# Hybrid decoder block on one core: two recurrence chains, three tile sets for combining the inverse's blocks, and an earlier load of the norm's weight

## The chip, the cores and the metric

The kernel runs on one core of one Trainium2 chip. The metric is the device time of one execution in microseconds; the time of a kernel is the median of its runs. The engines are named as the profile names them: PE multiplies matrices (PEld loads its weights), DVE works element by element, ACT does activations and copies, POOL does the rest of the elementwise work, and SP issues most of the DMA transfers.

## What is computed

One layer for 1024 tokens of width 1024. `h = rmsnorm(x)`, one projection `h @ w_in`, and three branches: a gated delta rule with 8 heads, stick-breaking attention with 8 heads, and a cross attention into 256 memory tokens with 4 heads. Each branch is projected to width 1024, the three are gated and added, and an output projection, the residual and a last norm follow.

The delta rule is what most of the change is about. Per head, in chunks of 64 tokens:

```python
t_inv = triangular_solve(eye + m, eye)          # m strictly lower triangular, 64 x 64
u = t_inv @ (v * beta);  w = t_inv @ (k * beta * exp(G))
a_intra = (q @ k.T) * gam_incl
def step(s, xs):                                # one chunk
    v_new = u_n - w_n @ s
    o = q_n @ s + a_n @ v_new
    s = s * exp(last_n) + k_n.T @ v_new
    return s, o
```

## The kernel before

All numbers are float32; matrices that need full precision are split into two parts, and a product is three matmuls (`mm3`, L156). The kernel joins two chunks into one of 128 tokens: it inverts the two 64x64 diagonal blocks of every chunk for all heads at once and adds the off-diagonal block from them. There are `NT` = 8 chunks of 128 tokens and `H` = 8 heads.

The stages, in order of time:

1. **Start, A.** Rows of x (128 tokens each) are loaded by `row` (L268), normed (`norm`, L273, whose last instruction, L284 on DVE, needs the norm's weight `g1`), transposed on PE (L292) and split (L143 on ACT, L144 on DVE). L364 to L372 set the order in which SP is given the first loads: rows 0 and 4 of x, two pieces of `wv0`, the weight `g1` broadcast to 128 partitions, two more pieces of `wv0`.
2. **Projections.** `stream` (L170) works through a list of jobs. Every `slot()` runs one unit of 12 matmuls; other work is put between the slots by generators and a `pacer` (L848), which calls a generator so often that it has done a given share of its steps. Beside the projections run `solver` (the 64x64 inverses, on DVE), `memory` (the cross attention) and `combine`.
3. **combine (L742).** For each head: three loads into `t12` and `ct` (L747 to L749), eight small matmuls Y (L752), a scaling on DVE (L753), eight matmuls X (L758), a copy on ACT (L759) and a store (L760). The tiles carry the tags `tmp` and `T1` in a pool with one buffer each, so one set of tiles serves all heads in turn. Y and X share the PSUM tag `wk` (2 banks) with the scores and values of `memory`.
4. **Attention** with the rest of the projections between its parts.
5. **Merge.** `branch` (L1150) runs for the memory branch (`y_ym`, 8 times), the attention branch (`y_ysb`, 8 times) and the delta branch (`y_ydn`, 8 times). The recurrence is put between the matmuls of the first two: `beside3` is called 40 times and has `recurrence` do all its steps by then (`RECUR` = 65, `RP` = 1.05). What is left is called at `recur(2.0)` (L1200). `y_ydn` reads the results `odn` of the recurrence. `load_o(wout, ...)` (L1205) loads and splits the last weight, `wo`, beside it.
6. **Output** projection, residual and norm (L1213 on).

**recurrence (L765)** goes through chunks `n` and, in each, groups `g` of four heads. A step (n, g) has four parts with a `yield` after each:

- loads; `kS` = k times the state S (L801, PE), `vb` += r3 * kS (L803, DVE, four instructions)
- `Tr` = inverse times vb (L809, PE), copied to `vn` (L811, ACT)
- `o` from q and S (L816) and from the inner attention and vn (L817), then `dS` = k times vn (L821), then the new S on DVE (L824)
- the norm of o (L834 on ACT, L835 to L837 on POOL, L838 on DVE), transposes `oT` (L841), product with the gate `zt` (L842, DVE), split into `odn`

The two groups share no values, but the code runs group 0 and then group 1 of a chunk, and they share buffers: `kd`, `qd`, `zt`, `vn` and `sq` have one, `kt`, `vb` and `at` two, and the PSUM tag `wk` has three banks (L1188).

The order on each engine is fixed when the program is built (`TileContext(nc, schedule_with_timeline_sim=True)`, L1316); it is not the order of the source. In the profile, SP issues the load of L393 between those of L153.

Of the kernel before, what the change touches and what calls it, by code (L numbers as in the profile page):

```python
# [11 lines left out]
F32 = mybir.dt.float32  # L12
F32R = mybir.dt.float32r
AF = mybir.ActivationFunctionType
ALU = mybir.AluOpType
# [4 lines left out]
P = 128  # L20
T = 1024
NT = 8
KC = 8
H = 8
# [13 lines left out]
def hybrid_block(ctx, tc, x, mem, norm_g, mem_norm_g, wq, wv0, wba, convw, a_log, dt_bias,  # L38
# [17 lines left out]
    cst = pool("cst", 1)  # L56
# [25 lines left out]

    ident = cst.tile([P, P], F32, name="ident")
    make_identity(nc, ident)
    tri = cst.tile([P, P], F32, name="tri")
    gp.memset(tri, 1.0)
    gp.affine_select(out=tri, in_=tri, compare_op=ALU.is_ge, fill=0.0, base=0,
                     pattern=[[1, P]], channel_multiplier=-1)
    ones = cst.tile([P, P], F32, name="ones")
    gp.memset(ones, 1.0)  # L90
    mhalf = cst.tile([P, 8], F32, name="mhalf")
    gp.memset(mhalf, -0.5)
    cw = cst.tile([P, 24, 4], F32, name="cw")
# [174 lines left out]
    def row(src, tb):  # L268
        t = ap_.tile([P, T], F32, tag="xt", bufs=4, name=f"xt_{tb}")
        sy.dma_start(out=t, in_=src[0, tb * P:tb * P + P, :])  # L270
        return t
# [89 lines left out]
        sums("S1", "S2")  # L361
        return functools.partial(sums, "S3", "S4")

    rows_ = {tb: row(x, tb) for tb in (0, 4)}  # L364

    w0 = [vp_.tile([P, KC, 272], F32R, name=f"w0{j}") for j in "hl"]
    w0r = [raw_unit(f"v0_{j}", wv0[j]) for j in range(2)]
    g1 = ap_.tile([P, T], F32, name="g1")
    sy.dma_start(out=g1, in_=norm_g.rearrange("a b -> (a b)").partition_broadcast(P))
    w0r += [raw_unit(f"v0_{j}", wv0[j]) for j in range(2, 4)]  # L370
    rb = vp_.tile([P, KC, 16], F32, name="rb")
    sy.dma_start(out=rb, in_=wba.rearrange("p (a b) -> p a b", a=KC))  # L372
# [23 lines left out]
    v_st.close()  # L396


    beta, G, nG, eG, elast, dec = (tab(n) for n in ("beta", "G", "nG", "eG", "elast", "dec"))
    nr2, r1, r3, eq = tab("nr2"), tab("r1"), tab("r3"), tab("eq")  # L400
    SS = dict(c=None)

# [221 lines left out]
    def solver():  # L624
        vp = slv["pool"] = pool("solve", 1, side="right", stack=solve_st)
        o = psum("tr", "nr2T")
        pe.transpose(o[0:64, 0:P], nr2.rearrange("p h n -> p (h n)"), ident)
        nrs = vp.tile([64, P], F32, name="nrs")
        ve.tensor_copy(nrs, o[0:64, 0:P])
        for b in range(2):  # L630
            sy.dma_start(out=nr_d[b], in_=nrs[:, b * 64:b * 64 + 64])
        nrp = vp.tile([P, 64], F32, name="nrp")
        sy.dma_start(out=nrp, in_=nr_d.rearrange("b m i -> (b m) i"))

        M = vp.tile([P, 64, 64], F32, name="M")
        sy.dma_start(out=M, in_=md_d.rearrange("b h n j i -> (b h n) j i"))
        tmp = vp.tile([P, 1024], F32, name="tmp")
        yield
        for c in range(4):
            s = slice(c * 16, c * 16 + 16)  # L640
            ve.tensor_tensor(out=M[:, s, :], in0=M[:, s, :], in1=nrp.unsqueeze(1).to_broadcast([P, 16, 64]),
                             op=ALU.mult)
        gp.memset(M.rearrange("p k r -> p (k r)")[:, 0:4096:65], 1.0)
        yield
        for j in range(1, 63):
            b = 63 - j
            t = tmp[:, 0:j * b].rearrange("p (k r) -> p k r", k=j)
            ve.tensor_tensor(out=t, in0=M[:, 0:j, j].unsqueeze(2).to_broadcast([P, j, b]),  # L648
                             in1=M[:, j, j + 1:64].unsqueeze(1).to_broadcast([P, j, b]), op=ALU.mult)
            d = M[:, 0:j, j + 1:64]  # L650
            ve.tensor_tensor(out=d, in0=d, in1=t, op=ALU.add)  # L651
            yield
        gp.dma_start(out=td_d.rearrange("b h n j i -> (b h n) j i"), in_=M)
        for c in range(4):
            s = slice(c * 16, c * 16 + 16)
            t = vp.tile([64, 16, 64], F32, tag=("tmp", "T1")[c % 2], name=f"T1_{c}")
            ve.tensor_copy(t, M[0:64, :, s].rearrange("p k r -> p r k"))
            sy.dma_start(out=t1_d[:, :, s, :].rearrange("h n r k -> (h n) r k"), in_=t)
            yield
            yield  # L660
# [79 lines left out]
                yield  # L740

    def combine():  # L742
        vp = slv["pool"]
        for h in range(H):
            t, u = (vp.tile([P, 2, 512], F32, tag=n, name=f"{n}c_{h}") for n in ("tmp", "T1"))
            t12, ct, Y, X = (v.rearrange("p (n k) -> p n k", n=NT) for v in (t[:, 0], t[0:64, 1], u[:, 0], u[0:64, 1]))
            sy.dma_start(out=t12[0:64], in_=t1_d[h].rearrange("n r k -> r n k"))  # L747
            sy.dma_start(out=t12[64:P], in_=td_d[1, h].rearrange("n k r -> k n r"))
            sy.dma_start(out=ct, in_=mo_d[h])  # L749
            o = psum("wk", f"Y_{h}")  # L750
            for n in range(NT):
                pe.matmul(o[64:P, n * 64:n * 64 + 64], ct[:, n, :], t12[0:64, n, :], start=True, stop=True)  # L752
# [12 lines left out]
    def recurrence(ep, odn):  # L765
# [10 lines left out]
        def loads(n, g):  # L776
            kt = ld(kt_d, n, g, "kt") if n else None
            vb = ld(vb_d, n, g, "vb")
            tt, hs = tts[g], slice(g * 4, g * 4 + 4)
            for b in range(2):  # L780
                q = slice(b * 64, b * 64 + 64)
                sy.dma_start(out=tt[q, :, q], in_=td_d[b, hs, n].rearrange("h j i -> j h i"))
            sy.dma_start(out=tt[0:64, :, 64:P], in_=xx_d[n, :, hs, :])
            kd = ld(kd_d, n, g, "kd", 1) if n < NT - 1 else None
            qd = ld(qd_d, n, g, "qd", 1) if n else None
            at = ld(at_d, n, g, "at")
            zt = ep.tile([P, 4, P], F32, tag="zt", bufs=1, name=f"zt_{n}_{g}")
            sy.dma_start(out=zt, in_=zf_d[g * 4:g * 4 + 4, :, n * P:n * P + P].rearrange("h d t -> d h t"))
            return kt, vb, tt, kd, qd, at, zt

        ahead = loads(0, 0)
        yield
        for n in range(NT):
            for g in range(2):
                hs = range(4)
                kt, vb, tt, kd, qd, at, zt = ahead or loads(n, g)
                ahead = None
                if n:
                    o = psum("wk", f"kS_{n}_{g}")
                    for h in hs:  # L800
                        pe.matmul(o[:, h * P:h * P + P], kt[:, h, :], S[:, g * 4 + h, :], start=True, stop=True)  # L801
                    for h in hs:
                        ve.scalar_tensor_tensor(out=vb[:, h, :], in0=o[:, h * P:h * P + P],  # L803
                                                scalar=r3[:, g * 4 + h, n:n + 1], in1=vb[:, h, :],
                                                op0=ALU.mult, op1=ALU.add)
                    yield
                o = psum("wk", f"Tr_{n}_{g}")
                for h in hs:
                    pe.matmul(o[:, h * P:h * P + P], tt[:, h, :], vb[:, h, :], start=True, stop=True)  # L809
                vn = ep.tile([P, 4, P], F32, tag="vn", bufs=1, name=f"vn_{n}_{g}")  # L810
                sc.activation(vn, o.rearrange("p (h c) -> p h c", h=4), AF.Copy)  # L811
                yield
                oo = psum("wk", f"o_{n}_{g}")
                for h in hs:
                    if n:
                        pe.matmul(oo[:, h * P:h * P + P], qd[:, h, :], S[:, g * 4 + h, :], start=True, stop=False)  # L816
                    pe.matmul(oo[:, h * P:h * P + P], at[:, h, :], vn[:, h, :], start=(n == 0), stop=True)  # L817
                if n < NT - 1:
                    o = psum("wk", f"dS_{n}_{g}")
                    for h in hs:  # L820
                        pe.matmul(o[:, h * P:h * P + P], kd[:, h, :], vn[:, h, :], start=True, stop=True)  # L821
                    for h in hs:
                        if n:
                            ve.scalar_tensor_tensor(out=S[:, g * 4 + h, :], in0=S[:, g * 4 + h, :],  # L824
                                                    scalar=elast[:, g * 4 + h, n:n + 1],
                                                    in1=o[:, h * P:h * P + P], op0=ALU.mult, op1=ALU.add)
                        else:
                            ve.tensor_copy(S[:, g * 4 + h, :], o[:, h * P:h * P + P])
# [13 lines left out]
                ve.tensor_tensor(out=zt, in0=o.rearrange("p (h c) -> p h c", h=4), in1=zt, op=ALU.mult)  # L842
                split([t[:, g * 4:g * 4 + 4, n * P:n * P + P] for t in odn], zt)
                yield

    SOLVE, MEM, COMB, RECUR = 1 + 1 + 62 + 8, 40, 16, 1 + 16 * 4

# [62 lines left out]

    b_st = sub()
    bp = pool("B", 1, stack=b_st, side="right")
    def hn(t):
        return t.rearrange("p h n -> p n h")

# [405 lines left out]
```

## Time and profile before

| | |
|---|---|
| median of three runs | 1606.89 us (1605.71 to 1613.69) |
| profiled execution, its own time | 1605.6 us |
| its span in the profile | 1603.9 us |
| instructions | 23268 |
| mean granted TensorE clock | 0.991 |
| moved by DMA | 223.58 MB, 139 GB/s over the span |

How to read the views that follow. A row of a table of stretches gives, for a window of the span in us, its length, the busy time of PE, PEld, DVE, ACT and POOL with the number of instructions, the granted clock of PE as a share of full speed, the share of the DMA engines' time that was busy, and GB/s; the length less the PE time is PE's idle time. A row of the timeline gives start, duration, engine, line, operation, what is written and read, and in brackets how long the engine sat idle before and what ended that. A row of waits gives the engine and line that waited, for whom, the total in us, how often, and the longest.

### The profile page before, as it was taken

How to read it: one execution, taken by the hardware profiler on the slowest of the kernel's cores; microseconds unless marked ns; L12 is line 12 of the kernel's file. 1: busy time of each engine (PE TensorE's matmuls, PEld its weight loads, DVE VectorE, ACT ScalarE, POOL GpSimd, SP SyncE). 2: the span in 40 equal slices, each digit the busy share in tenths (PEclk: the TensorE clock that was granted, in tenths of full speed). 3: DMA queues.
4: the chain of work that ended last, by engine and by line, in shares of the span. 5: the costliest groups of instructions: out<-in, count | busy, mean ns of one | idle time of the engine just before them, and what ended most of it. 6: DMA issues, size and time to landing. Idle time of an engine off the chain costs nothing.

```text
span 1603.9 us, 23268 instructions
## 1 busy us (share of the span) xinstructions
PE 1532.3 (96%) x7979; PEld 1292.5 (81%) x7979; DVE 1179.0 (74%) x1903; ACT 817.3 (51%) x1909; POOL 315.4 (20%) x567
## 2 busy tenths in 40 slices
PE   6899999999999998998999999999998999989998
PEld 5888888887888777876888888888877888778786
DVE  7688989979999998654678778877876655544333
ACT  7578887765555346644555555555554222221111
POOL 4516435341123110000012111111211011010011
PEclk9999999999999999999999999999998999999999
DMA  8337546563334356433322322332148856644222
GB/s 297 93 101 229 155 155 189 161 216 96 110 105 118 132 188 200 129 105 99 109 88 81 104 98 80 98 112 88 52 156 274 265 182 195 192 131 138 73 105 79
DMA packets 152551, 223.58 MB, mean 139 GB/s; under 512 B 39920, under 2 KB 68336, under 8 KB 152176
## 3 DMA queue, kind: packets, MB, share of 16 engines
q1 hardware_dynamic: 107616, 160.20, 32.9%
q10 hardware_dynamic: 35712, 32.51, 6.1%
q0 software_dynamic: 9104, 29.37, 5.4%
q8 instruction: 63, 1.03, 0.3%
q14 instruction: 56, 0.46, 0.1%
HBM read 150.63 MB, written 71.40 MB: 138 GB/s over the span
## 4 chain that ended last, share of the span: by engine, by line
PE 62%; DMA 5%; DVE 4%; issue 4%; ACT 2%; POOL 1%; SPq 0%; POOLq 0%; DVEq 0%; ACTq 0%
PE mmY_g L160 3%; PE mmY_g L162 3%; PE mmY_g L161 3%; PE mmY_skq L160 2%; PE mmY_skq L162 2%; PE mmY_skq L161 2%; PE out L1229 2%; PE out L1227 2%; PE out L1228 2%; PE y_ydn L1161 2%; PE y_ydn L1162 2%; PE y_ydn L1163 2%; PE aTp L1059 2%; PE y_ysb L1161 2%; PE y_ysb L1163 2%
## 5 line engine op out<-in xcount | busy, mean ns | idle before, releaser
L1033 DVE TENSOR_TENSOR_SCAN pf<-pf 128x512 f32<-128x512 f32 (+4 forms) x96 | 97.2, 1013 | 15.7 <-POOL pf L1031 15.6
L143 ACT ACTIVATE aTh<-aTp 128x512 fp32r<-128x512 f32 (+2 forms) x96 | 44.8, 498 | 57.4 <-PE aTp L1059 54.2
L144 DVE TENSOR_TENSOR aTl<-aTp,aTh 128x512 fp32r<-128x512 f32 (+2 forms) x96 | 50.6, 547 | 23.1 <-ACT aTh L143 23.1
L1018 POOL MEMSET pf<- 128x1 f32 x64 | 6.0, 98 | 312.6 <-PE aTp L1059 180.8
L1031 POOL TENSOR_SCALAR_AFFINE_SELECT pf<-pf 128x128 f32<-128x128 f32 x64 | 25.7, 402 | 196.6 <-ACT pf L1027 196.6
L1027 ACT ACTIVATE pf<-z 128x512 f32<-128x512 f32 (+4 forms) x96 | 47.1, 498 | 31.4 <-PE z L162 27.4
L1036 DVE TENSOR_TENSOR pf<-be,pf 128x512 f32<-128x512 f32 (+4 forms) x96 | 53.8, 560 | 3.8
L651 DVE TENSOR_TENSOR M<-M,tmp 128x62 f32<-128x62 f32 (+30 forms) x62 | 53.6, 865 | 0.2
L648 DVE TENSOR_TENSOR tmp<-M 128x62 f32<-128x62 f32 (+30 forms) x62 | 53.3, 860 | 0.1
L1227 PE MATMUL out<-oh_wo,mh 128*128 128x512 f32 x128 | 50.0, 391 | 1.5 <-ACT mh L143 1.5
L1161 PE MATMUL y_ydn<-odnh,w_ydn 128*128 128x512 f32 x128 | 49.5, 391 | 1.7 <-ACT odnh L143 1.7
L1161 PE MATMUL y_ysb<-oh_sb,w_ysb 128*128 128x512 f32 x128 | 50.7, 396 | 0.3 <-DVE mer L1169 0.3
L1163 PE MATMUL y_ysb<-oh_sb,w_ysb 128*128 128x512 f32 x128 | 50.5, 395 | 0.0
L1162 PE MATMUL y_ysb<-ol_sb,w_ysb 128*128 128x512 f32 x128 | 50.3, 393 | 0.0
L1163 PE MATMUL y_ydn<-odnh,w_ydn 128*128 128x512 f32 x128 | 49.9, 390 | 0.0
L1162 PE MATMUL y_ydn<-odnl,w_ydn 128*128 128x512 f32 x128 | 49.8, 389 | 0.0
L1228 PE MATMUL out<-ol_wo,mh 128*128 128x512 f32 x128 | 49.8, 389 | 0.0
L1028 ACT ACTIVATE be<-z 128x512 f32<-128x512 f32 (+4 forms) x96 | 47.2, 503 | 4.4 <-DVE pf L1036 4.4
L1229 PE MATMUL out<-oh_wo,ml 128*128 128x512 f32 x128 | 49.3, 389 | 0.0
L1075 PE MATMUL av<-aTl,vh 128*128 128x256 f32 (+1 forms) x160 | 47.0, 294 | 2.3 <-DVE aTl L144 2.3
L1074 PE MATMUL av<-aTh,vh 128*128 128x256 f32 (+1 forms) x160 | 45.2, 283 | 3.3 <-ACT aTh L143 3.3
L1234 DVE TENSOR_TENSOR xo<-out,xo 128x512 f32<-128x512 f32 x16 | 11.1, 692 | 48.0 <-PE out L1229 48.0
(816 smaller groups left out, 5514.9 us busy)
## 6 DMA issues: line engine op xcount, KB each, us to landing
wb_g_b<-in_wq_dram SPq DMA_DIRECT2D x48, 256.0 KB, 3.1
wb_kq_b<-in_wq_dram SPq DMA_DIRECT2D x32, 256.0 KB, 3.0
wb_skq_b<-in_wq_dram SPq DMA_DIRECT2D x32, 256.0 KB, 2.7
g_d<-g ACTq DMA_DIRECT2D x32, 256.0 KB, 2.0
xt<-in_x_dram SPq DMA_DIRECT2D x8, 512.0 KB, 4.8
wb_sz_b<-in_wq_dram SPq DMA_DIRECT2D x16, 256.0 KB, 3.5
kt_d<-kq ACTq DMA_DIRECT2D x16, 256.0 KB, 3.4
gam<-gr_d SPq DMA_DIRECT2D x8, 512.0 KB, 4.2
```

The source lines that it names most:

```text
L160: pe.matmul(o, ah, bh, start=(first and i == 0), stop=False, **kw)
L161: pe.matmul(o, ah, bl, start=False, stop=False, **kw)
L162: pe.matmul(o, al, bh, start=False, stop=(i == n - 1), **kw)
L651: ve.tensor_tensor(out=d, in0=d, in1=t, op=ALU.add)
L1033: ve.tensor_tensor_scan(out=pv[:, ::-1], data0=pv[:, ::-1], data1=pv[:, ::-1], initial=pf[:, off + c1:off + c1 + 1], op0=ALU.mult, op1=ALU ...
L1036: ve.tensor_tensor(out=d, in0=be, in1=d, op=ALU.mult)
L1161: pe.matmul(oo[hf], wh, oh[:, s], start=(k == 0), stop=False)
L1162: pe.matmul(oo[hf], wh, ol[:, s], start=False, stop=False)
L1163: pe.matmul(oo[hf], wl, oh[:, s], start=False, stop=(k == n - 1))
L1227: pe.matmul(oo[hf], mh[:, k, :], wo[k][0][:, s], start=(k == 0), stop=False)
L1228: pe.matmul(oo[hf], mh[:, k, :], wo[k][1][:, s], start=False, stop=False)
L1229: pe.matmul(oo[hf], ml[:, k, :], wo[k][0][:, s], start=False, stop=(k == KC - 1))
```

## The change

- **Recurrence.** The loop over `n` and `g` becomes a generator `chain(g)` with a loop over `n` alone. Two of them, for the heads 0 to 3 and 4 to 7, are advanced in turn, one part each; chain 1 runs two parts behind chain 0. `dS` is given to PE ahead of `o`. `zt` has two buffers in place of one. Chunk 0 has one more `yield` per group, so there are 65 parts in place of 63. All other buffer counts stay, and every instruction stays.
- **combine.** Three sets of tiles, made once: the tags `tmp` and `T1`, and two halves of a tile that takes the place of the solver's `M` once that is done with. The loads of head h+1 are given out ahead of the matmuls of head h.
- **Start.** The load of `g1` stands right behind that of row 0 of x, ahead of row 4.
- **Room.** `tri` and `ones` (three POOL instructions) are made later, in the pool `B` of the decay stage; `G` and `nG` lie in the memory of `bat`, which has been read by then.

```diff
-    rows_ = {tb: row(x, tb) for tb in (0, 4)}
+    rows_ = {0: row(x, 0)}
+    g1 = ap_.tile([P, T], F32, name="g1")
+    sy.dma_start(out=g1, in_=norm_g.rearrange("a b -> (a b)").partition_broadcast(P))
+    rows_[4] = row(x, 4)
 
     w0 = [vp_.tile([P, KC, 272], F32R, name=f"w0{j}") for j in "hl"]
     w0r = [raw_unit(f"v0_{j}", wv0[j]) for j in range(2)]
-    g1 = ap_.tile([P, T], F32, name="g1")
-    sy.dma_start(out=g1, in_=norm_g.rearrange("a b -> (a b)").partition_broadcast(P))
...
     def combine():
+
         vp = slv["pool"]
-        for h in range(H):
-            t, u = (vp.tile([P, 2, 512], F32, tag=n, name=f"{n}c_{h}") for n in ("tmp", "T1"))
+        room = vp.tile([P, 4, 2, 512], F32, tag="M", name="Mc")
+        sets = [[vp.tile([P, 2, 512], F32, tag=n, name=f"{n}c") for n in ("tmp", "T1")],
+                [room[:, 0], room[:, 1]], [room[:, 2], room[:, 3]]]
+
+        def operands(h):
+            t, u = sets[(h + 1) % 3]
             t12, ct, Y, X = (v.rearrange("p (n k) -> p n k", n=NT) for v in (t[:, 0], t[0:64, 1], u[:, 0], u[0:64, 1]))
             sy.dma_start(out=t12[0:64], in_=t1_d[h].rearrange("n r k -> r n k"))
             sy.dma_start(out=t12[64:P], in_=td_d[1, h].rearrange("n k r -> k n r"))
             sy.dma_start(out=ct, in_=mo_d[h])
+            return t12, ct, Y, X
+
+        nxt = operands(0)
+        for h in range(H):
+            (t12, ct, Y, X), nxt = nxt, operands(h + 1) if h < H - 1 else None
...
-            zt = ep.tile([P, 4, P], F32, tag="zt", bufs=1, name=f"zt_{n}_{g}")
+            zt = ep.tile([P, 4, P], F32, tag="zt", bufs=2, name=f"zt_{n}_{g}")
...
-        ahead = loads(0, 0)
-        yield
-        for n in range(NT):
-            for g in range(2):
-                hs = range(4)
+        def chain(g, ahead=None):
+            hs = range(4)
+            for n in range(NT):
...
-                    yield
+                yield
...
+                if n < NT - 1:
+                    o = psum("wk", f"dS_{n}_{g}")
+                    for h in hs:
+                        pe.matmul(o[:, h * P:h * P + P], kd[:, h, :], vn[:, h, :], start=True, stop=True)
                 oo = psum("wk", f"o_{n}_{g}")
...
-                    o = psum("wk", f"dS_{n}_{g}")
-                    for h in hs:
-                        pe.matmul(o[:, h * P:h * P + P], kd[:, h, :], vn[:, h, :], start=True, stop=True)
...
+        first_loads = loads(0, 0)
+        yield
+        two = chain(0, first_loads), chain(1)
+        for i in range(4 * NT + 2):
+            for g in (1, 0):
+                if 0 <= i - 2 * g < 4 * NT:
+                    next(two[g])
+                    yield
```

More of the change, by code (lines that the diff above doesn't have):

```diff
@@ L84, in hybrid_block @@
     make_identity(nc, ident)
[L85 to L90, printed above, removed]
     mhalf = cst.tile([P, 8], F32, name="mhalf")
@@ L396, in hybrid_block @@
     v_st.close()
-    beta, G, nG, eG, elast, dec = (tab(n) for n in ("beta", "G", "nG", "eG", "elast", "dec"))
+    beta, eG, elast, dec = (tab(n) for n in ("beta", "eG", "elast", "dec"))
+    G, nG = (bat.rearrange("p n c -> p (n c)")[:, j * 64:j * 64 + 64].rearrange("p (h n) -> p h n", h=H)
+             for j in range(2))
     nr2, r1, r3, eq = tab("nr2"), tab("r1"), tab("r3"), tab("eq")
@@ L633, in solver @@
         sy.dma_start(out=nrp, in_=nr_d.rearrange("b m i -> (b m) i"))
-        M = vp.tile([P, 64, 64], F32, name="M")
+        M = vp.tile([P, 64, 64], F32, tag="M", name="M")
         sy.dma_start(out=M, in_=md_d.rearrange("b h n j i -> (b h n) j i"))
@@ L912, in hybrid_block @@
     bp = pool("B", 1, stack=b_st, side="right")
+    tri = bp.tile([P, P], F32, name="tri")
+    gp.memset(tri, 1.0)
+    gp.affine_select(out=tri, in_=tri, compare_op=ALU.is_ge, fill=0.0, base=0,
+                     pattern=[[1, P]], channel_multiplier=-1)
+    ones = bp.tile([P, P], F32, name="ones")
+    gp.memset(ones, 1.0)
     def hn(t):
```

## The prediction, made blind

> **What bounds the kernel now.** I read the page's engine totals first, then a table of stretches, then PE's waits, then the timeline at each place where PE stood still.
>
> ```profile
> PE 1532.3 (96%) x7979; PEld 1292.5 (81%) x7979; DVE 1179.0 (74%) x1903; ACT 817.3 (51%) x1909; POOL 315.4 (20%) x567
> 0.00:10.00 10.00, 0.00 (x0) 0.00 (x0) 2.03 (x3) 4.73 (x7) 2.75 (x14) 1.00 0.82 268
> 10.00:60.00 50.00, 42.19 (x303) 40.01 (x304) 49.56 (x76) 37.80 (x73) 27.47 (x30) 0.93 0.68 230
> 590.00:640.00 50.00, 43.37 (x202) 33.98 (x201) 44.72 (x86) 28.57 (x68) 0.96 (x1) 1.00 0.67 205
> 700.00:740.00 40.00, 31.35 (x209) 24.94 (x208) 18.01 (x34) 18.67 (x45) 0.00 (x0) 0.91 0.38 101
> 740.00:1190.00 450.00, 449.49 (x2392) 383.67 (x2391) 344.12 (x533) 239.36 (x493) 63.01 (x177) 1.00 0.29 92
> 1190.00:1220.00 30.00, 22.42 (x117) 18.93 (x117) 25.98 (x44) 15.49 (x36) 5.03 (x17) 0.83 0.85 273
> 1385.00:1426.00 41.00, 30.69 (x211) 27.58 (x210) 22.68 (x52) 12.96 (x53) 7.27 (x15) 0.96 0.58 170
> 1500.00:1603.90 103.90, 95.19 (x418) 77.89 (x416) 34.65 (x45) 19.39 (x41) 9.60 (x24) 0.99 0.24 87
> ```
>
> PE is the bound: busy 1532.3 of 1603.9 us, and over long stretches (740 to 1190) idle for 0.5 us in 450. The change takes no matmul away, so it can only win the 71.6 us in which PE is idle and the time in which PE runs at a lower granted clock. The rows say where the idle time is: 10.0 us before the first matmul, 7.8 in 10 to 60, 6.6 in 590 to 640 (cross attention), 8.65 in 700 to 740 (combine), 7.6 in 1190 to 1220 (end of the attention), 10.3 in 1385 to 1426 (end of the recurrence), 8.7 at the end. The change speaks to the first two, the fourth and the sixth. I take them in turn.
>
> **The start.** g1 goes ahead of row 4 and of two pieces of wv0.
>
> ```profile
> 0.80 0.87 SPq L270 DMA_DIRECT2D xt<-in_x_dram  x2
> 2.65 0.43 SPq L369 DMA_DIRECT2D g<-in_norm_g_dram  x1
> 4.31 1.06 ACT L277 ACTIVATE sq_x<-xt 128x1024 bf16<-128x1024 f32 x1 [2.23 <-DMA xt<-in_x_dram]
> 5.62 1.06 ACT L277 ACTIVATE sq_x<-xt 128x1024 bf16<-128x1024 f32 x1 [0.17 <-DMA xt<-in_x_dram]
> 5.82 0.56 POOL L280 TENSOR_TENSOR rs_x<-rs_x,mhalf 128x1 f32<-128x1 f32 x1
> 7.32 1.35 DVE L144 TENSOR_TENSOR w0l<-wb_v,w0h 128x512 fp32r<-128x512 f32 x2 [7.32 <-ACT w0h L143]
> 9.32 2.48 DVE L284 SCALAR_TENSOR_TENSOR xt<-xt,rs_x,g 128x1024 f32<-128x1024 f32 x2 [0.65 <-DMA g<-in_norm_g_dram]
> 10.09 1.34 ACT L143 ACTIVATE w0h<-wb_v 128x512 fp32r<-128x512 f32 x2 [2.14 <-DMA wb_v<-in_wv_dram]
> 10.66 3.28 PEld L292 LDWEIGHTS xT_x<-ident,xt 128*128 128x128 f32 x16 [10.66 <-DVE xt L284]
> ```
>
> The loads land in the order of their issue: row 0 at 4.31, row 4 by 5.62, g1 at 9.32, the third piece of wv0 at 10.09. From 5.62 to 10.09 landed 1280 KB (three pieces of 256 and g1 with 512), so 512 KB take about 1.8 us. Behind row 0, g1 lands at about 4.31 + 1.8 = 6.1; the norm's factor is ready at 5.82 + 0.56 = 6.38; the first L284 can start near 6.5 in place of 9.32, 2.8 us earlier. But row 4 and the first pieces of wv0 come 1.8 us later, and with them the second L284 (from squares to factor row 0 takes 4.31 to 6.38, 2.1 us; 5.62 + 1.8 + 2.1 = 9.5, against 10.56 now) and w0l (7.32 becomes 9.1). Then DVE decides: from 10 to 60 it is busy for 49.56 of 50 us. By 10.0 it has done 2.03 us of work now; after the change its one sure piece is the first L284, half of 2.48, 1.24 us. Ends: -0.8 us (that work is missing) and +2.8 (all else follows the first row). I take **0.5**, since DVE's row is the nearest. The Trainium skill ("Trainium Kernel Development and Optimization", Key Constraints) says that the DMAs of all issuing queues run on the same 16 DMA engines and interleave. By that a load put first only puts others back, and the sum would have 0 here; the order of landing above agrees.
>
> **Combine.** Now one set of tiles serves all heads, so the loads of a head start when X of the head before has been read.
>
> ```profile
> 713.28 0.59 SPq L747 DMA_DIRECT2D tmpc<-t_d  x1
> 718.72 1.11 PE L752 MATMUL Y<-tmpc 64*64 64x64 f32 x16 [2.09 <-DMA tmpc<-mo_d]
> 725.41 0.94 PE L712 MATMUL mT<-ident,pt 128*128 128x128 f32 x4 [1.08 <-ACT pt L700]
> 729.73 1.93 PE L752 MATMUL Y<-tmpc 64*64 64x64 f32 x16 [3.38 <-DMA tmpc<-mo_d]
> 730.00:736.00 6.00, 6.00 (x41) 5.09 (x40) 1.72 (x4) 1.92 (x6) 0.00 (x0) 0.60 0.00 0
> ```
>
> From the issue of the three loads to Y pass 718.72 - 713.28 = 5.4 us. In two heads nothing else was left for PE in that time: it waited 2.09 and 3.38 us, 5.5 together, and the six us behind the longer wait ran at a clock of 0.60, which costs 6 x 0.40 = 2.4. With three sets the loads go out one head ahead; a head takes 729.73 - 718.72 = 11 us, which covers the 5.4 twice. So 5.5 + 2.4 = 7.9 us go. What is late next is the softmax of the cross attention, which shares two PSUM banks with Y and X (the wait of 1.08 on ACT). I leave one such wait more, 1.1, and some at lower clock: **6.5**. Ends: 0 (PE waits there for the softmax anyway) and 8.65 + 2.4 = 11. The Trainium skill ("TensorE: Matmul & The Clock Gate", Why this matters for your kernels) wants no idle gap over about 3 us between matmuls. The trace agrees: the wait of 2.09 left the clock alone, that of 3.38 did not. By that rule, removing the shorter gap brings 2.1 and the longer one its clock as well, the same 7.9. The loads on SP are the same 24; they wait less behind X, so weight loads queued behind them lose nothing.
>
> **The recurrence.** Two rows of PE's groups in 1262 to 1380, then one step of the timeline.
>
> ```profile
> L1161 PE MATMUL y_ysb<-oh_sb,w_ysb 128*128 128x512 f32 x114 | 44.9, 394 | 0.0
> L809 PE MATMUL Tr<-vb,tt 128*128 128x128 f32 x64 | 9.6, 277 | 0.6 <-DVE vb L803 0.6
> 1260.00:1380.00 120.00, 118.95 (x701) 104.50 (x700) 63.05 (x138) 29.30 (x98) 11.64 (x24) 1.00 0.66 202
> 1315.87 1.06 PE L801 MATMUL kS<-S,kt 128*128 128x128 f32 x8
> 1321.78 0.83 PE L809 MATMUL Tr<-vb,tt 128*128 128x128 f32 x6
> 1328.12 0.38 PE L817 MATMUL o<-vn,at 128*128 128x128 f32 x2
> 1330.57 1.06 PE L801 MATMUL kS<-S,kt 128*128 128x128 f32 x8
> ```
>
> A step takes 1330.57 - 1315.87 = 14.7 us, and eight of them (64 Tr at 8 a step) fill 1262 to 1380. PE is idle for only 1.05 us there, because y_ysb fills two pauses in each step: behind kS (DVE makes vb) and behind Tr (ACT makes vn), about 5 us each. So nothing is won in this stretch itself. But kS of the next step always comes right behind o and dS of the last: the groups go one after the other. When y_ysb runs out at 1385, four of the 16 Tr are still to come (the first at 1394.72, the last at 1418.28), with little to put into their pauses: the 24 matmuls of y_ydn that need the early chunks alone.
>
> ```profile
> 1384.91 0.39 PE L1161 MATMUL y_ydn<-odnh,w_ydn 128*128 128x512 f32 x1
> 1394.72 1.26 PE L809 MATMUL Tr<-vb,tt 128*128 128x128 f32 x8 [0.83 <-DVE vb L803]
> 1399.88 0.49 PE L817 MATMUL o<-vn,at 128*128 128x128 f32 x2 [3.08 <-ACT vn L811]
> 1400.00:1405.00 5.00, 5.00 (x30) 4.93 (x30) 2.09 (x6) 1.77 (x9) 0.66 (x3) 0.66 0.29 88
> 1415.06 0.49 PE L816 MATMUL o<-S,qd 128*128 128x128 f32 x2 [1.88 <-DMA qd<-qd_d]
> 1418.28 1.06 PE L809 MATMUL Tr<-vb,tt 128*128 128x128 f32 x8
> 1420.93 0.49 PE L816 MATMUL o<-S,qd 128*128 128x128 f32 x2 [1.60 <-DMA qd<-qd_d]
> 1425.17 0.73 PE L1161 MATMUL y_ydn<-odnh,w_ydn 128*128 128x512 f32 x2 [1.75 <-ACT odnh L143]
> ```
>
> This end costs 41 - 30.69 = 10.3 us idle and 5 x 0.34 = 1.7 us of clock, 12.0.
>
> With two chains two parts apart the order on PE becomes: dS and o of chain 1, kS of chain 0, pause, Tr of 0 and kS of 1, pause, dS and o of 0, Tr of 1, pause. Three pauses for two steps in place of four; the other fell under work of the other chain. y_ysb is used up at 3/4 of the amount per step. The nine Tr from 1262 to 1385 become about twelve, so one step or so is left at 1385 in place of four. I take two thirds of 12.0 as won, **8**; left are the last norm, transposes and split (1.75) and what waits for qd and for ACT. Ends: 0 and 12. That dS is ahead of o wins nothing by itself: the new S must still wait until o has read the old one. The second zt is 2 KB of room, its load off the path. The extra yields in chunk 0 move nothing else. tri and ones are three POOL instructions on an engine that is 20% busy, four slots ahead of their use; G and nG come behind the last read of bat. All these: 0; without cover, under 1 us.
>
> **The sum.** 0.5 + 6.5 + 8 = 15.0 us from the profiled execution's own 1605.6: 1590.6. That execution was 1.3 us below the median of 1606.9, so the forecast for the median is **1592 us**.
>
> **Rivals.** (1) Slower: the buffers become the wait. kd and qd keep one buffer for both chains.
>
> ```profile
> kd<-kd_d SPq DMA_DIRECT2D x13, 256.0 KB, 5.0
> qd<-qd_d SPq DMA_DIRECT2D x13, 256.0 KB, 3.1
> ```
>
> kd of chain 1 can only be loaded once dS of chain 0 has read it. Between two dS now pass about 14 us; then it is o, one Tr and one pause. o and dS take 1328.12 to 1330.57, 2.5 us, of which o has some 1.5; Tr is about as long as kS, 1.06; with a pause of 5 that is 7.5 us, against 5.0 of landing. It decides where landing plus the queue on SP pass 7.5 us. If each of the seven pairs then stalls PE for the longest DMA wait seen (3.38), that is 24 us against a gain of 7 from the other parts: 1606.9 + 17 = 1624. For it: DMA is already busy for 66% there. A step loads seven tiles of about 256 KB, eight steps 14 of the 24 MB (202 GB/s for 120 us); a third more of that makes it about 79%. Against: in 1260 to 1380 PE waited 1.05 us in all. Chance 0.08. (2) The end of the recurrence stays: ACT and DMA, full with wo, hold vn up just as before (the 3.08), and only combine pays: 1606.9 - 7 = 1600. Or combine's gap only moves to the softmax, and the end pays: 1606.9 - 8.5 = 1598. Together 0.22. (3) Nothing shows, because the new order on each engine opens gaps of the same size elsewhere, as in 590 to 640 or 1190 to 1220, whose 6.6 and 7.6 us no line of the change explains: 1602 to 1610, 0.10. (4) All three places are emptied: 2.8 + 11 + 12 = 26, 1581, 0.14. The forecast, 1586 to 1598: 0.46.
>
> **How the numbers follow.** About 8 us (0.5%) is what a measurement of this kernel can tell from no change, so faster means below 1598.9. The forecast, (4) and 0.08 of (2) lie there: 0.68. Same: 0.14 of (2) and (3), 0.24. Slower: 0.08. The range from 1580 to 1607 takes in the forecast, (2), nearly all of (4) and most of (3).
>
> **What the profile after would show.** The first L284 near 6.5 without a wait on g1; if the first v matmul still starts where it did, the 0.5 is right. No wait of Y on a DMA, PE's idle time in combine down from 8.65 to about 3. Two steps of the recurrence in about 25 us in place of 29, steady y_ydn some 10 us sooner after the end of y_ysb. I am wrong if PE waits on kd or qd within the recurrence, or if PE's total idle time stays near 72 us.

## The result and the profile after

| | before | after |
|---|---|---|
| median | 1607.8 us (6 runs, 1605.6 to 1613.7) | 1583.1 us (6 runs, 1579.3 to 1585.3) |
| ratio to before, 95% interval | | 0.984 [0.9817, 0.9862] |
| profiled execution, its own time | 1605.6 us | 1579.32 us |
| its span | 1603.9 us | 1577.6 us |

The kernel became faster by 24.7 us, 1.6%. The forecast was 1592 us with a range of 1580 to 1607; the time lies in the range, 9 us below the forecast and below the 1586 to 1598 that it took as its own band, and next to the rival in which all three places are emptied (1581). One execution of the kernel with the two chains alone took 2193.81 us at a granted clock of 0.653; its ratio leaves that one out, and without it its median is 1594.11 in place of the 1596.0 given below.

The engine totals of the page of after, and the stretches that answer to those of before:

```profile
PE 1526.8 (97%) x7979; PEld 1291.4 (82%) x7979; DVE 1181.4 (75%) x1903; ACT 817.8 (52%) x1909; POOL 318.0 (20%) x567
0.00:10.00 10.00, 1.97 (x8) 1.57 (x8) 1.69 (x2) 4.54 (x8) 2.21 (x11) 1.00 0.76 281
10.00:60.00 50.00, 43.47 (x292) 41.39 (x293) 48.54 (x75) 36.25 (x71) 26.27 (x29) 0.90 0.70 231
590.00:640.00 50.00, 43.67 (x206) 34.48 (x205) 46.45 (x92) 30.81 (x74) 1.49 (x1) 1.00 0.65 195
700.00:740.00 40.00, 39.08 (x276) 31.97 (x275) 21.44 (x38) 20.74 (x46) 0.00 (x0) 1.00 0.38 100
1180.00:1210.00 30.00, 23.25 (x112) 19.64 (x113) 24.61 (x42) 14.08 (x33) 5.04 (x14) 0.77 0.87 270
1390.00:1400.00 10.00, 10.00 (x56) 8.62 (x55) 6.05 (x10) 2.71 (x11) 2.31 (x3) 1.00 0.33 105
1400.00:1480.00 80.00, 80.00 (x357) 66.26 (x356) 35.24 (x55) 16.20 (x26) 0.00 (x0) 1.00 0.36 112
1480.00:1577.60 97.60, 88.90 (x390) 72.67 (x388) 34.64 (x45) 19.39 (x41) 9.60 (x24) 0.98 0.26 92
```

PE still has its 7979 matmuls. Its idle time went from 71.6 to 1577.6 - 1526.8 = 50.8 us, 20.8 less, and its busy time from 1532.3 to 1526.8, 5.5 less: 26.3 us of span in all. The idle time of 700 to 740 went from 8.65 to 0.92 us and its clock from 0.91 to 1.00. The hole behind the end of `y_ysb` (10.3 us idle in 1385 to 1426) is gone: from 1390 to 1480 PE never stands still. Most of what is left stands where it stood before: the first 60 us, cross attention (6.3 in 590 to 640), the end of the attention (6.75 in 1180 to 1210, now at a clock of 0.77), and the last 100 us (8.7).

To split the 26.3 us by stage, three stretches of each kernel, cut at the same marks: the first `mmY_mq`, the first `z`, the first `y_ym` and the first `out`. They are combine, attention and merge. Before, then after:

```profile
555.30:782.60 227.30, 210.70 (x1134) 169.70 (x1133) 157.16 (x269) 114.60 (x249) 7.65 (x15) 0.98 0.48 144
782.60:1216.00 433.40, 425.64 (x2271) 365.38 (x2269) 343.41 (x535) 233.94 (x493) 67.84 (x192) 0.99 0.31 101
1216.00:1508.60 292.60, 277.73 (x1522) 238.39 (x1520) 153.02 (x305) 77.65 (x226) 24.72 (x48) 0.99 0.58 180
```

```profile
556.90:775.50 218.60, 210.62 (x1157) 171.98 (x1156) 159.47 (x274) 117.93 (x253) 8.18 (x15) 1.00 0.52 152
775.50:1203.90 428.40, 421.02 (x2247) 361.65 (x2247) 339.67 (x531) 231.29 (x489) 68.73 (x192) 0.99 0.32 101
1203.90:1482.30 278.40, 273.52 (x1521) 235.87 (x1521) 155.38 (x305) 78.10 (x226) 24.20 (x48) 0.99 0.61 189
```

Combine and attention have to be read together, since 23 matmuls of the projections went from the second into the first (x1134 became x1157): together 660.7 became 647.0, 13.7 less. Merge is 14.2 less. What lies ahead of the first mark is 1.6 longer (556.9 against 555.3), what lies behind the last is the same (95.3 in both). So -13.7 - 14.2 + 1.6 = -26.3, and the question of the experiments is whether the two places are independent, and which edit pays in each.

### The profile page after: what moved, and what is told of

It is laid out like the page before. It is cut to its first block, busy times and chain, and to the rows that moved or that the text cites. A ratio compares the mean times of both kernels' runs of the same rounds, so it can differ in the third digit from the quotient of the medians.

```text
span 1577.6 us, 23271 instructions
## 1 busy us (share of the span) xinstructions
PE 1526.8 (97%) x7979; PEld 1291.4 (82%) x7979; DVE 1181.4 (75%) x1903; ACT 817.8 (52%) x1909; POOL 318.0 (20%) x567
## 4 chain that ended last, share of the span: by engine, by line
PE 79%; DVE 6%; issue 5%; DMA 4%; ACT 3%; POOL 2%; SPq 0%; DVEq 0%; POOLq 0%; ACTq 0%
PE mmY_g L154 3%; PE mmY_g L156 2%; PE mmY_g L155 2%; PE mmY_skq L154 2%; PE y_ydn L1186 2%; PE y_ydn L1185 2%; PE out L1252 2%; PE y_ydn L1184 2%; PE out L1250 2%; PE out L1251 2%; PE mmY_skq L155 2%; PE mmY_skq L156 2%; PE aTp L1082 2%; PE y_ysb L1184 2%; PE y_ysb L1186 2%
## 5 line engine op out<-in xcount | busy, mean ns | idle before, releaser
L138 DVE TENSOR_TENSOR aTl<-aTp,aTh 128x512 fp32r<-128x512 f32 (+2 forms) x96 | 50.8, 548 | 24.1 <-ACT aTh L137 24.1
L1054 POOL TENSOR_SCALAR_AFFINE_SELECT pf<-pf 128x128 f32<-128x128 f32 x64 | 29.1, 455 | 196.4 <-ACT pf L1050 196.4
```

## The experiments

Medians, with the ratio to the kernel before measured in the same series (its medians are 1608.7 and 1608.8 us). The kernels fall into three groups: parts of the change put into the kernel before, the change with one part undone, and the smallest set of edits that pays.

**One part alone: the two chains.** The kernel before with the chains, `dS` ahead of `o`, the second `zt` and the moved tables; combine and the start stay.

```diff
-        for n in range(NT):
-            for g in range(2):
-                hs = range(4)
+        def chain(g, ahead=None):
+            hs = range(4)
+            for n in range(NT):
...
+        for i in range(4 * NT + 2):
+            for g in (1, 0):
+                if 0 <= i - 2 * g < 4 * NT:
+                    next(two[g])
+                    yield
```

> The two recurrence chains alone (with the moved tables that make room for the second zt buffer); combine and the order of the first loads are those of the kernel before. Theory (each part empties its own place): 12 to 15 us faster than before, since the recurrence stage is 14.6 us shorter in the changed kernel, and PE idle below 1.5 us between the last y_ysb and the first steady y_ydn. Rival (the end empties only because the combine stage let the merge start earlier or because the three parts work together): under 6 us.

Measured: 1596.0 us, 0.9917 [0.9898, 0.9937]: 13.4 us less than before (10 to 16). In its trace `y_ydn` starts at 1412.6, right behind the last `y_ysb` at 1412.3, as the theory had it.

**One part alone: combine.** The kernel before with the three sets of tiles and their loads written one head ahead, and nothing else.

```diff
+        room = vp.tile([P, 4, 2, 512], F32, tag="M", name="Mc")
+        sets = [[vp.tile([P, 2, 512], F32, tag=n, name=f"{n}c") for n in ("tmp", "T1")],
+                [room[:, 0], room[:, 1]], [room[:, 2], room[:, 3]]]
...
+            (t12, ct, Y, X), nxt = nxt, operands(h + 1) if h < H - 1 else None
```

> The three sets of tiles and the loads one head ahead in combine alone; the rest is the kernel before. Theory: 10 to 14 us faster, no wait of Y on a DMA, and the stretch from the first cross-attention scores to the last attention score shorter by that. Rival (the idle time moves to the end of the attention, which is reached earlier with nothing left to fill it): under 6 us, with the lost time in the last 30 us before the merge.

Measured: 1595.96 us, 0.9927 [0.9909, 0.9944]: 11.7 us less (9 to 15).

**One part alone: the start.** The kernel before with `g1` right behind row 0.

```diff
-    rows_ = {tb: row(x, tb) for tb in (0, 4)}
+    rows_ = {0: row(x, 0)}
+    g1 = ap_.tile([P, T], F32, name="g1")
+    sy.dma_start(out=g1, in_=norm_g.rearrange("a b -> (a b)").partition_broadcast(P))
+    rows_[4] = row(x, 4)
```

> The norm's weight loaded right behind row 0 alone. Theory (DVE decides from 10 us on, and a load put first puts others back): within 2 us of before either way, first transposes near 7.9 us in place of 10.7, but the projections reach the solver's first transpose at the same time. Rival (the start is a chain and all that follows moves with it): 2.8 us faster.

Measured: 1605.49 us, 0.9984 [0.9969, 0.9999]: 2.6 us less (0.2 to 5.0).

**One part alone: the moved tables.** The kernel before with `tri` and `ones` made later and `G` and `nG` in the memory of `bat`.

```diff
-    beta, G, nG, eG, elast, dec = (tab(n) for n in ("beta", "G", "nG", "eG", "elast", "dec"))
+    beta, eG, elast, dec = (tab(n) for n in ("beta", "eG", "elast", "dec"))
...
+    tri = bp.tile([P, P], F32, name="tri")
...
+    ones = bp.tile([P, P], F32, name="ones")
```

> Only the tables moved: tri and ones made later in the decay stage, G and nG in the memory of bat. Theory: within 1 us of before. Rival (the three POOL instructions or the shared memory hold up the decay stage): 1 to 3 us slower, seen as a later first transpose of the solver (352 in place of 350 us).

Measured: 1609.88 us, 1.001 [0.9995, 1.0026]: no difference.

What follows from these four: the chains and combine each pay about half, and 13.4 + 11.7 = 25.1 is the whole of the change within the errors. Within these errors the two places don't feed on each other. The stretch of combine shows the switch; it is the first row in the kernel with the chains alone, the second in that with combine alone:

```profile
700.00:740.00 40.00, 32.04 (x210) 25.50 (x210) 16.87 (x30) 14.47 (x34) 0.00 (x0) 0.90 0.34 89
```

```profile
700.00:740.00 40.00, 38.77 (x270) 31.88 (x270) 21.66 (x39) 21.73 (x50) 0.00 (x0) 1.00 0.38 101
```

The sets alone take 6.7 us of idle time and the lower clock (0.90) out of these 40 us. Here are PE's waits from 690 to 745, first in the kernel with the chains alone, then in that with combine alone (columns: who waited and where, for whom, total, times, longest):

```profile
PE Y L749 <- DMA tmpc<-mo_d: 5.2, 2, 3.4
PE X L755 <- ACT pt L693: 1.1, 1, 1.1
PE mT L709 <- ACT pt L697: 1.1, 1, 1.1
```

```profile
PE X L768 <- ACT pt L696: 0.9, 1, 0.9
```

Not only the two waits of Y on the DMA went, but also one of the two on the softmax (`pt`). The softmax was to be late next; it came sooner instead. Y and X share two PSUM banks with the scores, so while Y stood waiting for its loads, a score that wanted the bank behind it may have stood too. That this is the reason was not tested by itself; that the wait went with the sets is in the rows.

**The change, chains a whole step at a time.** All of the change stays (two buffers of `zt`, `dS` ahead of `o`, sets, start), but chain 0 does all four parts of a step before chain 1 does its four, as the kernel before did.

```diff
-        for i in range(4 * NT + 2):
-            for g in (1, 0):
-                if 0 <= i - 2 * g < 4 * NT:
+        for n in range(NT):
+            for g in range(2):
+                for _ in range(4):
                     next(two[g])
                     yield
```

> The changed kernel with the two chains advanced a whole step at a time (four parts of chain 0, then four of chain 1), as the loop before did; dS ahead of o and the second zt buffer stay. Theory (three pauses a pair in place of four): most of the recurrence's gain is lost, 10 to 14 us slower than the changed kernel, 10 to 14 us faster than before; a pair of steps takes 28 to 30 us again and y_ysb ends before the recurrence. Rival (the second zt buffer or the order of dS and o makes the gain): within 4 us of the changed kernel.

Measured: 1592.27 us, 0.9898 [0.9877, 0.9918], 9.2 us above the change, whose interval it doesn't touch. So it is the turns of the two chains that pay. The theory asked for a little more, 10 to 14 us: 9.2 is less than the 13.4 of the chains alone, and with intervals of some 3 us to each side the traces don't say whether another edit carries part of the rest. PE's timeline in the recurrence, first of the change, then of this kernel:

```profile
1300.10 1.05 PE L822 MATMUL dS<-vn,kd 128*128 128x128 f32 x8
1303.21 1.06 PE L807 MATMUL kS<-S,kt 128*128 128x128 f32 x8
1308.89 1.05 PE L815 MATMUL Tr<-vb,tt 128*128 128x128 f32 x8
1309.78 0.39 PE L807 MATMUL kS<-S,kt 128*128 128x128 f32 x2
1314.31 1.05 PE L822 MATMUL dS<-vn,kd 128*128 128x128 f32 x8
1316.99 1.06 PE L815 MATMUL Tr<-vb,tt 128*128 128x128 f32 x8
1323.13 1.05 PE L822 MATMUL dS<-vn,kd 128*128 128x128 f32 x8
```

```profile
1300.61 1.06 PE L807 MATMUL kS<-S,kt 128*128 128x128 f32 x8
...
1314.88 1.06 PE L807 MATMUL kS<-S,kt 128*128 128x128 f32 x8
...
1328.93 1.06 PE L807 MATMUL kS<-S,kt 128*128 128x128 f32 x8
```

In the change `Tr` of one chain and `kS` of the other stand back to back (1308.89 and 1309.78), and a pair of steps takes 1323.13 - 1300.10 = 23.0 us. In turn it takes 1328.93 - 1300.61 = 28.3. PE is full in both (30.00 of 30.00 us in 1300 to 1330); what differs is how much `y_ysb` a step uses up while it waits. The view of one tile shows what that decides (count, duration min/median/max in ns, first and last start). Last `Tr` and last `y_ysb` of the change, then of the kernel in turn:

```profile
L815 PE MATMUL Tr<-vb,tt x128: 271/275/275, 1211.1 to 1385.8; 128*128 128x128 f32 x128
L1186 PE MATMUL y_ysb<-oh_sb,w_ysb x128: 387/389/478, 1240.3 to 1393.3; 128*128 128x512 f32 x128
```

```profile
L815 PE MATMUL Tr<-vb,tt x128: 271/275/377, 1210.0 to 1399.6; 128*128 128x128 f32 x128
L1186 PE MATMUL y_ysb<-oh_sb,w_ysb x128: 387/389/478, 1239.0 to 1374.3; 128*128 128x512 f32 x128
```

The kernel before:

```profile
L809 PE MATMUL Tr<-vb,tt x128: 270/275/377, 1220.3 to 1419.1; 128*128 128x128 f32 x128
L1163 PE MATMUL y_ysb<-oh_sb,w_ysb x128: 388/389/478, 1252.1 to 1384.7; 128*128 128x512 f32 x128
```

In the change the last `Tr` stands 7.5 us ahead of the last `y_ysb`; in turn it stands 25.3 us behind, and before 34.4 us behind (1419.1 against 1384.7). Whatever of the recurrence stands behind has little cover. The other traces agree: in all nine kernels whose chains take turns the last `Tr` stands ahead of the last `y_ysb`, by 3.5 to 14.9 us, and in all five without turns behind it, by 25.3 to 36.3.

**The change, chain 1 one part behind** in place of two, to bring the two chains' use of `kd` and `qd` together.

```diff
-        for i in range(4 * NT + 2):
+        for i in range(4 * NT + 1):
...
-                if 0 <= i - 2 * g < 4 * NT:
+                if 0 <= i - g < 4 * NT:
```

> The changed kernel with chain 1 one part behind chain 0 in place of two. dS of chain 1 then follows dS of chain 0 with only o and one pause between, so the one kd buffer has the least time to be loaded again. Theory (the buffers would become the wait where landing passes the gap, the rival of the prediction): a pair of steps takes 1 to 4 us longer, PE waits for kd or qd 1 to 4 us in all, the whole 1 to 6 us slower than the changed kernel. Rival (y_ysb fills whatever the loads need, at any lag): within 1 us of the changed kernel.

Measured: 1583.72 us, 0.9848 [0.9827, 0.9869], as the change. PE's waits in 1200 to 1480, the change first, then this kernel:

```profile
PE dS L822 <- DMA kd<-kd_d: 1.4, 1, 1.4
PE o L826 <- DMA qd<-qd_d: 0.5, 1, 0.5
```

```profile
PE o L826 <- DMA qd<-qd_d: 2.6, 2, 1.8
PE dS L822 <- DMA kd<-kd_d: 2.1, 2, 1.4
```

The waits that rival (1) spoke of exist: 1.9 us in the change, 4.7 with the chains closer. They are far from the 24 us of the prediction's rival, and too small to measure in the time. The theory of this run missed: the kernel is 0.6 us above the change in place of 1 to 6, and its steps are no longer, since from the first `Tr` to the last pass 170.7 us (1211.6 to 1382.3), against 174.7 in the change. Work of `y_ysb` covers the loads at this lag too.

**The change, `dS` behind `o`.**

```diff
-                if n < NT - 1:
-                    o = psum("wk", f"dS_{n}_{g}")
...
                 oo = psum("wk", f"o_{n}_{g}")
...
+                if n < NT - 1:
+                    o = psum("wk", f"dS_{n}_{g}")
```

> The changed kernel with dS given to PE behind o again, as in the kernel before; all else as changed. Theory (the turns of the two chains make the gain): within 3 us of the changed kernel, so 22 to 28 us faster than before, 23 us for a pair of steps. Rival (dS ahead of o frees the only kd buffer 2 us sooner, and its load decides): 6 us or more slower than the changed kernel, with PE waiting for kd.

Measured: 1580.11 us, 0.9822 [0.9802, 0.9843], as the change.

**The change, one buffer of `zt`** (`bufs=2` becomes `bufs=1`).

> The changed kernel with one buffer for zt, as before. Theory: the last parts of the two chains lie half a pair, some 11 us, apart, a load of zt takes 4 us to land, so within 3 us of the changed kernel. Rival (the one zt holds the last part of a chain until the other has been split, and with it the banks of o): 6 us or more slower, a pair of steps over 25 us.

Measured: 1582.57 us, 0.9842 [0.9822, 0.9863], as the change.

**The change, loads of combine not ahead.** The three sets stay, but the loads of a head are written right in front of its own matmuls.

```diff
-        nxt = operands(0)
...
-            (t12, ct, Y, X), nxt = nxt, operands(h + 1) if h < H - 1 else None
+            t12, ct, Y, X = operands(h)
```

> The changed kernel with three sets of tiles in combine, but the loads of a head written right before its own matmuls, not one head ahead. Theory (what held the loads up was the one set of tiles; with three nothing holds them, and SP, which is idle, issues them early by itself): within 3 us of the changed kernel. Rival (being written one head ahead is what hides them): 5 us or more slower than the changed kernel, with PE waiting for mo_d again.

Measured: 1579.75 us, 0.9823 [0.9802, 0.9844], as the change. The reason stands in SP's timeline beside PE's, first of the change, then of this kernel:

```profile
648.45 1.28 SPq L750 DMA_DIRECT2D Mc<-t_d  x2
649.78 0.63 SPq L750 DMA_DIRECT2D tmpc<-t_d  x1
...
689.79 0.57 PE L760 MATMUL Y<-tmpc 64*64 64x64 f32 x7
690.38 0.57 SPq L750 DMA_DIRECT2D tmpc<-t_d  x1
...
719.90 1.14 PE L760 MATMUL Y<-tmpc 64*64 64x64 f32 x16
```

```profile
688.28 0.92 PE L759 MATMUL Y<-tmpc 64*64 64x64 f32 x13
689.23 0.57 SPq L750 DMA_DIRECT2D tmpc<-t_d  x1
```

In the change the loads of the first three heads are out by 653. From then on the operands of Y are loaded again as soon as Y has read them (Y at 689.79, the load at 690.38), and the Y that needs this load comes 29 us later, at 719.90. In the kernel of this run the same load stands right behind the same Y (688.28 and 689.23). The program's builder placed these loads where their tiles come free, not where the source has them; with three sets that is three heads ahead in both ways of writing.

**The change, two sets in place of three** (`sets[(h + 1) % 3]` becomes `sets[(h + 1) % 2]`).

> The changed kernel with two sets of tiles in combine in place of three. Theory (a head takes some 10 us, its loads 5.4 us from issue to use): two sets hide them as well, within 3 us of the changed kernel, no wait of Y on a DMA. Rival (the loads of a head must wait until the one before the last has been read and stored, and that is too late): 4 us or more slower, Y waits for mo_d again.

Measured: 1579.49 us, 0.9831 [0.9807, 0.9855], as the change. In its trace no Y waits on a DMA: two sets cover the 5.4 us from load to Y already.

**The change with the start of before.**

> The changed kernel with the loads of the start in the order of before. Theory (the start is decided by DVE, g1 ahead brings nothing): within 2 us of the changed kernel either way, the first projection of keys and queries ends at the same time. Rival (the 2.6 us that the start alone showed are real): 2 to 4 us slower than the changed kernel.

Measured: 1583.36 us, 0.9835 [0.981, 0.9861], as the change. The start alone gave 2.6 us (0.2 to 5.0), its removal changes nothing (the intervals of both kernels are 3.6 us or more to each side): whether it is worth 0 or 3 us is not decided.

**Two edits only.** The kernel before with the turns of the chains (`dS` behind `o`, one `zt`, no moved tables) and the three sets (loads not ahead, start of before).

```diff
+            t, u = sets[(h + 1) % 3]
...
+            t12, ct, Y, X = operands(h)
...
+        two = chain(0, first_loads), chain(1)
+        for i in range(4 * NT + 2):
+            for g in (1, 0):
+                if 0 <= i - 2 * g < 4 * NT:
```

> The kernel before with two edits alone: the two chains advanced in turn two parts apart (dS behind o, one buffer for zt) and three sets of tiles in combine (loads written right before their own matmuls). The first loads, tri, ones, G and nG are as before. Theory (these two carry the gain): 22 to 28 us faster than before, within 3 us of the changed kernel. Rival (the small edits carry some of it together): 5 us or more slower than the changed kernel.

Measured: 1582.1 us, 0.9835 [0.9812, 0.9858], as the change. These two edits carry all of the gain that can be measured. The traces of all fourteen kernels, cut at the marks above, say the same. Combine and attention together last 659.6 to 663.8 us in the four kernels with one set and 647.0 to 652.1 in the ten with more, whatever the chains do; merge lasts 287.7 to 300.3 us in the five kernels without turns and 277.5 to 282.5 in the nine with them, whatever the sets do. No kernel here is measurably faster than the change: the lowest medians (1579.5, 1579.8, 1580.1) lie within its interval.

## Why the prediction was right, and where it was off

**PE bounds the kernel; only its idle time and clock can be won.** Right: the same 7979 matmuls, 20.8 us less idle and 5.5 us less busy time. The two main mechanisms were right; their sizes were not. The sum was 15.0 us and the measured gain 24.7, with both main terms too small, and the range took the time in because it left room for rival (4).

**Start, 0.5.** The first of the changed kernel's rows answers the first landmark:

```profile
6.55 1.28 DVE L278 SCALAR_TENSOR_TENSOR xt<-xt,rs_x,g 128x1024 f32<-128x1024 f32 x1 [6.55 <-DMA g<-in_norm_g_dram]
9.60 0.69 DVE L138 TENSOR_TENSOR w0l<-wb_v,w0h 128x512 fp32r<-128x512 f32 x1 [1.76 <-ACT w0h L137]
10.21 1.28 DVE L278 SCALAR_TENSOR_TENSOR xt<-xt,rs_x,g 128x1024 f32<-128x1024 f32 x1
13.16 0.57 PE L154 MATMUL v<-w0h,hA11h 128*128 128x272 f32 x1
```

The norm starts at 6.55 (forecast 6.5), but still on the landing of `g`: "without a wait on g1" was wrong, g1 is just what it waits for. The other side came much as worked out: `w0l` at 9.60 (forecast 9.1), the second norm at 10.21, 0.35 sooner than before (forecast 9.5). The first v matmul starts at 13.16 in place of 13.99, so it did not stay where it was, and the 0.8 us is not seen later: by 60 us PE has done 300 matmuls in place of 303 (the first two rows of the tables), with a clock of 0.90 in place of 0.93 from 10 to 60, and the first mark stands at 556.9 against 555.3. Over all the traces that mark stands at 555.3 on average in the eight kernels with `g1` ahead (554.1 to 557.3) and at 556.0 in the six without (554.9 to 558.2). That is near 0.5 and speaks against most of the 2.6 being won by then, but it is within the scatter. The 0.5 was neither refuted nor shown: the medians of the two kernels that bear on it leave open whether it is 0 or 3.

**Combine, 6.5.** The mechanism was right (no wait of Y on a DMA is left, the clock is 1.00); the size was not. The term measured 11.7 alone, at its upper end of 11. What failed is "I leave one such wait more, 1.1, and some at lower clock" and the 3 us of idle time left: 0.92 is left, as the waits on the softmax (690 to 745) shrank from 2.2 to 0.9 us when those of Y went. They were taken for a second limit behind the first; the runs show that one of the two leaves with it. In the profile, this stretch won 8.65 - 0.92 = 7.7 us of idle time and 31.35 x (1.00 - 0.91) = 2.8 of clock, 10.5. The Trainium skill ("TensorE: Matmul & The Clock Gate", Why this matters for your kernels) names gaps of over about 3 us as what lowers the clock, and here the trace agrees: with a wait of 3.4 left in, the clock of 700 to 740 is 0.90, without it 1.00.

"The loads go out one head ahead; a head takes 11 us, which covers the 5.4 twice" had the right conclusion from a wrong picture. The loads go out as soon as a set is read, up to 29 us ahead of their use; the edit that writes them ahead brings nothing that can be measured, and with a second set the whole gain is there.

**Recurrence, 8.** The order of PE came as written out (`dS` and `o` of one chain, `kS` of the other, then `Tr` beside `kS`), and "nothing is won in the stretch itself" held. The size was off: 13.4 (10 to 16) for the chains alone, where 8 was taken and 12.0 was the upper end. What failed is "one step or so is left at 1385": it counts the steps up to 1385 as if `y_ysb` still ended there. The pair came out at 23.0 us, where about 25 was forecast, from 29.4. Two things follow from a shorter pair: the recurrence ends sooner, and `y_ysb` lasts longer, since the same amount spreads over more steps. Counted from the first `y_ym`, the last `Tr` came 21 us sooner (181.9 in place of 203.1) and the last `y_ysb` 21 us later (189.4 in place of 168.7). Together they moved the last `Tr` from 34.4 us behind the end of `y_ysb` to 7.5 us ahead, so that no step is left, and the last norm and the waits for `qd` and ACT (the 1.75 and the rest that was to stay) have cover as well. All 10.3 us of idle time went. The busy time of merge fell by 4.2 besides: 1.7 is the clock. The other 2.5 were not taken apart; a part of them is that a `Tr` right behind a pause took 1.26 us before (1394.72) and one without a pause 1.06 (1418.28).

The steady `y_ydn` was forecast some 10 us sooner behind the end of `y_ysb`. It begins at 1393.6, right behind the last `y_ysb` at 1393.3, without a pause, where before the last pause ended at 1425.17, 40 us behind 1384.9: some 40 us sooner, not 10.

**The edits at 0.** The order of `dS` and `o`, the second `zt` and the moved tables were put at nothing; the three kernels that undo or isolate them agree with it to some 3 us each.

**The rivals.** (1) `kd` and `qd`: there, at 1.9 us in place of 24. By its words the prediction's sign of being wrong (PE waits on `kd` or `qd` within the recurrence) came up, but the sign was badly chosen: the kernel before waited for them too, for 4.4 us (3.5 for `qd`, 0.9 for `kd`). The longest such wait in the traces with turns is 3.8, once, in the kernel of two edits; nowhere does it come in each pair. (2) Only one place pays: refuted by the two parts alone. (3) Gaps open elsewhere: those of 590 to 640 and of the attention's end are as large as before (6.3 and 6.75), no larger by more than the profiles differ. (4) All three emptied, 1581: nearest to the truth. Two of the three are as good as empty and gave about their upper ends (11.7 and 13.4 against 11 and 12, within their intervals); what the start gave, of its 2.8, is open. It had 0.14 because each of the two main terms was made smaller for something behind it, the softmax and the last step, that was to stay and went too.

## What to carry to other kernels

Where independent chains of work have pauses, advance them in turn, part by part: here the gain was not in the stretch in which other work fills the pauses anyway, but in whether the chains end before that work runs out. Read both ends off the first and last start of each tile, and move both when you price the change. Where the builder orders loads by when their tiles come free, the number of sets counts, not where the source writes the load; try two before three. A short wait next to a removed one, on work that shares its PSUM banks, can be a consequence of it and need not be the next limit.

## What the runs showed of the hardware that was not expected

The granted clock fell without a long gap. At the end of the attention of the changed kernel (table of stretches, then four waits from PE's timeline, all that exceed 0.3 us between 1184 and 1198):

```profile
1186.00:1190.00 4.00, 2.75 (x16) 1.77 (x14) 3.73 (x6) 4.00 (x10) 1.71 (x6) 1.00 0.99 292
1190.00:1193.00 3.00, 2.79 (x14) 2.65 (x13) 3.00 (x6) 0.04 (x1) 0.22 (x1) 0.57 0.97 275
1198.00:1204.00 6.00, 4.82 (x21) 4.12 (x21) 4.62 (x10) 2.86 (x6) 0.00 (x0) 0.50 0.72 232
```

```profile
1186.89 0.90 PE L1082 MATMUL aTp<-ident,pf 128*128 128x128 f32 x5 [0.32 <-DVE aTl L138]
1189.59 0.33 PE L154 MATMUL z<-kh,qh 128*128 128x128 f32 x1 [0.66 <-ACT be L1051]
1195.93 0.39 PE L1097 MATMUL av<-aTh,vh 128*128 128x256 f32 x1 [0.98 <-ACT aTh L137]
1197.75 0.58 PE L1098 MATMUL av<-aTl,vh 128*128 128x256 f32 x1 [1.43 <-DVE aTl L138]
```

Four microseconds with PE busy for 2.75, and no single wait above 0.66, were followed by a clock of 0.57. The Trainium skill ("TensorE: Matmul & The Clock Gate", A second HAM failure mode: psum-queue depth-cycling) describes a kernel in which frequent very short pauses between groups of matmuls make the clock swing. These rows fit that, and the rule of a 3 us gap alone does not cover them; no run here takes the pauses away to test it.

Single executions differ by several us in a stage that the edit doesn't touch: the merge stage of the kernel with the start alone, cut at the same marks, is 300.3 us long (the row below), that of the kernel before 292.6, with the same matmuls (x1522):

```profile
1214.70:1515.00 300.30, 281.57 (x1522) 242.51 (x1521) 154.11 (x307) 77.71 (x226) 24.38 (x48) 0.97 0.57 178
```

So the lengths of stages in one profile say where time went, and the medians say how much.
